# A group norm unit that loads three streams: centred values and a bonus made in the projections

## The chip, the cores and the metric

The kernel runs on one core of a Trainium2 chip. The metric is the device time of one execution in microseconds (us), the median of three runs.

## The reference

One layer of a bidirectional encoder over 1024 tokens of width 1024: a SwiGLU FFN, a mixing layer, and a second FFN, each between RMS norms. The mixing layer projects once and splits into eight attention heads and eight RWKV-7 heads of 64 features. The RWKV part, cut to what matters here:

```python
u = u + mu_prev * (prev - u) + mu_next * (nxt - u)
r, k, v, wd, ad, gd = split(u)
a = sigmoid(a0 + einsum('bsdr,drc->bsdc', ad, a2))          # two directions d
g = sigmoid(gd) @ g2
kk = normalised(k * k_k)                                     # per head
k_dir = k[:, :, None, :] * (1.0 + (a - 1.0) * k_a)
ys = scan(step, state0, (r, decay, k_dir, v, kk, kk * a))    # forward and backward
#   sa = state @ kk;  state = state * w - sa kka^T + v k^T;  y = state @ r
y = ys[:, :, 0] + flip(ys[:, :, 1])
mu = mean(y); var = mean((y - mu) ** 2)                      # per head of 64
y = (y - mu) * rsqrt(var + GN_EPS) * lnx_w + lnx_b
bonus = einsum('bshn,bsdhn,hn->bsh', r, k_dir, r_k) / 2
y = (y + bonus * v) * g
```

The state's rows belong to the value features, and the output of a head is linear in its values. So a value that has its mean over the 64 features taken away ahead of the scan gives an output that has its mean taken away.

## The kernel before

All data is feature-major where a name has `[128, 2, FB]` or `[4, 128, S]`: 128 partitions hold two heads of 64, four such pairs make the eight heads, and tokens run along the row. Instructions are placed on each engine's queue by a scheduler that works from its own cost model and the order of the program as priority; each queue then runs strictly in that order on the chip. SP's queue carries most loads and stores, POOL's (gpsimd) some stores, ACT's a few. A tile of a pool is reused after all its readers are done; `bufs` says how many copies a tag has.

The stages, in the order of the program:

1. First FFN, low-rank projections (decay and in-context rate, stored in `lr_d["w"]` and `lr_d["a"]` per direction, the backward one stored in its own, reversed order of time), values of the attention.
2. Attention, on `ps_a` and `attw`. Behind it in priority stand the projections of `project_rwkv`, column tile by column tile (`ct`): 0 to 3 are receptances r, 4 to 7 keys k, 8 to 11 values v. Each makes 48 products into the PSUM tile `zr`, is shifted (`shift`, tiles `u` and `us`) and goes through `stream`. `ct` 0 is done earlier; then the list is 4, 5, 6, 7, 1, 2, 3. A key's stream squares it, sums per head by small products (`kn`), takes a root and a reciprocal, spreads that by a copy, transposes it back (`kt`) and stores k and the normalised kk. r, k and kk lie together in `rk_d[12]`. A value's stream stores v for the bonus (`v_d`) and, both in order and reversed (`vrev`), transposes it with the identity and stores it token-major in `vt_d` by way of the tile `vts`, which has two buffers.
3. `prep(n)` makes the operands of one block of 128 tokens in both directions: it loads the block's decay and rate (`th_w`, `th_a`) and all twelve rows of `rk_d` in one DMA (`in3`, one buffer), makes `pr`, `bk`, `lm` and `bt`, and stores the direction's key `kd` to `kd_d`. `solve(n)` inverts small triangular matrices on VectorE, step by step in tile `Ti` (lines 866 and 868). prep(0), solve(0), values 8 and 9, prep(1), solve(1), values 10 and 11 follow one another in the program.
4. The scan: `merge` and `chain` for eight blocks of two chunks, with prep and solve of later blocks and the output projection of the attention (`project_attended`) between them. A chunk's output goes to `y_d`.
5. `finish_half` for two halves of two blocks of 256 tokens, each with two units (`finish_unit`, g = 0, 1): a unit covers four heads and 256 tokens. It loads seven tiles (`f_y0`, `f_y1`, `f_k0`, `f_k1`, `f_r`, `f_v`, `f_sg`, shown in views as f_y, f_k, f_r, f_v, f_sg), three buffers each, from a pool that opens when the last prep and solve are done. It adds both directions, centres by a product with `cen` (`yc`), squares, sums (`var`), takes the root, spreads and transposes it (`rstd`), makes the bonus from k, r and v (`bonus`), the gate (`gate`), and writes the unit's result as two parts, high and low (`xh`, `xl`). Its PSUM tiles come from one tag with three buffers.
6. `out_weights` loads eight 256 KB blocks of the output weights through the single buffer `wor` and splits each into `woh` (ACT) and `wol` (VectorE). `out_project` multiplies (`pw`) and `done` normalises each row tile, stores it, and hands it to the second FFN. These steps stand behind stage 5 in priority, but run as their operands come.
7. Second FFN.

Of the kernel before, what the change touches and what calls it, by code (L numbers as in the profile page):

```python
# [10 lines left out]
F32 = mybir.dt.float32  # L11
F32R = mybir.dt.float32r
AF = mybir.ActivationFunctionType
OP = mybir.AluOpType
# [149 lines left out]
class _Kernel:  # L164
# [401 lines left out]
    def stream(self, p, psum, ct, y):  # L566
# [10 lines left out]
        elif ct < 8:  # L577
# [15 lines left out]
            for half in range(2):  # L593
# [5 lines left out]
                V.scalar_tensor_tensor(kr[:, o], y[:, o], g, q, op0=OP.mult, op1=OP.mult)  # L599
            self.nc.gpsimd.dma_start(self.rk_d[8 + i], kr)  # L600
        else:
            i = ct - 8
            self.nc.gpsimd.dma_start(self.v_d[i], y)
            back = p.tile([128, S], F32, name="vrev", tag="us")
            V.tensor_copy(back, y[:, ::-1])
            for src, dst in ((y, self.vt_d[0]), (back, self.vt_d[1])):
                for g in range(2):
                    q = psum.tile([128, 4, 128], F32, name="vt", tag="t")
                    for j in range(4):
                        t = g * 4 + j  # L610
                        T.transpose(q[:, j, :], src[:, t * 128:(t + 1) * 128], self.ident)
                    vt = p.tile([128, 4, 2, 64], F32, name="vts", tag="vts")
                    A.activation(vt.rearrange("p a b c -> p a (b c)"), q, AF.Copy)
# [169 lines left out]
    def prep(self, n, p, psum, big):  # L783
# [8 lines left out]
        for d in range(2):  # L792
# [29 lines left out]
            V.tensor_tensor(bk[:, :, :, C:2 * C], chunks(kd), ei, op=OP.mult)  # L822
            self.nc.sync.dma_start(self.kd_d[d][:, :, ls].rearrange("a p t -> p a t"), kd)
            bt = big.tile([128, BLK, 2, 4, 64], F32, name="bt", tag=f"bt{d}")
# [149 lines left out]

    def finish_unit(self, p, psum, b, g, x, g2w):

        nc, V, A, G, T = self.nc, self.nc.vector, self.nc.scalar, self.nc.gpsimd, self.nc.tensor
        pos = self.blocks.index(b)
        half, cols = pos // 2, slice(pos % 2 * FB, pos % 2 * FB + FB)
        ps2, ts = slice(2 * g, 2 * g + 2), slice(b * FB, (b + 1) * FB)  # L980
        back = slice(S - (b + 1) * FB, S - b * FB)
        z = {}
        for nm, src, sl in (("y0", self.y_d[0], ts), ("y1", self.y_d[1], back), ("k0", self.kd_d[0], ts),
                            ("k1", self.kd_d[1], back), ("r", self.rk_d, ts), ("v", self.v_d, ts)):
            z[nm] = p.tile([128, 2, FB], F32, name="f_" + nm, tag="f_" + nm)
            self.load(z[nm], src[ps2, :, sl].rearrange("a p t -> p a t"))
        sg = p.tile([128, FB], F32, name="f_sg", tag="f_sg")
        self.load(sg, self.sg_d[:, ts])
        y, sq, k, v = z["y0"], z["y1"], z["k0"], z["v"]
        flat = lambda q: q.rearrange("p a t -> p (a t)")  # L990
        bank = lambda nm: psum.tile([128, 2, FB], F32, name=nm, tag="d")

        yc = bank("yc")
        G.tensor_tensor(y, y, z["y1"][:, :, ::-1], op=OP.add)
        T.matmul(yc, self.cen, y, start=True, stop=True)
        A.activation(sq, yc, AF.Square)
        G.tensor_tensor(k, k, z["k1"][:, :, ::-1], op=OP.add)
        for j in range(2):
            V.scalar_tensor_tensor(k[:, j, :], k[:, j, :], self.rkc[:, 2 * g + j:2 * g + j + 1], z["r"][:, j, :],
                                   op0=OP.mult, op1=OP.mult)  # L1000
# [11 lines left out]
        rb = bank("rstd")  # L1012
        for u in range(4):
            T.transpose(flat(rb)[:, u * 128:(u + 1) * 128], flat(sq)[:, u * 128:(u + 1) * 128], self.ident)
        A.activation(y, yc, AF.Copy)
        V.tensor_tensor(y, y, rb, op=OP.mult)
        for j in range(2):
            i = 2 * g + j
            A.activation(y[:, j, :], y[:, j, :], AF.Identity, scale=self.lnw[:, i:i + 1], bias=self.lnb[:, i:i + 1])
        V.scalar_tensor_tensor(v, bs, 0.5, v, op0=OP.mult, op1=OP.mult)  # L1020
        V.tensor_tensor(y, y, v, op=OP.add)
        gt = bank("gate")
        for j in range(2):
            i = 2 * g + j
            T.matmul(gt[:, j, :], g2w[:, i * 128:(i + 1) * 128], sg, start=True, stop=True)
# [9 lines left out]
    def finish_half(self, p, psum, half, x):  # L1035
        g2w = self.load_g2(p)
        for b in self.blocks[2 * half:2 * half + 2]:
            for g in range(2):
                self.finish_unit(p, psum, b, g, x, g2w)

# [58 lines left out]
    def constants(self):  # L1099
# [17 lines left out]
        self.sg_d = self.dram("sg", [128, S])  # L1117
        self.rk_d, self.v_d = self.dram("rk", [12, 128, S]), self.dram("v", [4, 128, S])
        self.q_d, self.kt_d = self.dram("q", [4, 128, S]), self.dram("kt", [4, 128, S])
        self.vt_d = self.dram("vt", [2, S, 2, 4, 64])  # L1120
        self.kd_d = [self.dram(f"kd{d}", [4, 128, S]) for d in range(2)]
        self.y_d = [self.dram(f"y{d}", [4, 128, S]) for d in range(2)]
# [3 lines left out]
    def mix_columns(self):  # L1126
# [36 lines left out]
    def run(self):  # L1163
# [5 lines left out]
        with self.top as top:  # L1169
# [266 lines left out]
```

## Time and profile before

| | |
|---|---|
| Median of three runs | 2369.29 us (2369.18 to 2370.75) |
| Span of the profiled execution, first to last instruction | 2367.7 us, 39507 instructions |
| TensorE busy | 2212.2 us, 93% |
| VectorE busy | 1782.8 us, 75% |
| ScalarE busy | 1034.4 us, 44% |
| GpSimd busy | 608.7 us, 26% |
| DMA | 386.04 MB, mean 163 GB/s |

The profile holds one execution. Its own time is known by its span alone; 1.6 us of the median lie outside that span. A row of the timeline has start, duration, engine, line, operation and tiles (out<-in), and in brackets how long the engine stood idle before it and what released it. PE is TensorE's matmul, PEld its weight load, DVE is VectorE, ACT ScalarE, POOL GpSimd, and SPq or ACTq a DMA issued from that queue. A row of the windows table has the stretch, its length, the busy time of PE, PEld, DVE, ACT and POOL with the number of instructions, the granted TensorE clock, the DMA engines' busy share and GB/s. A row of a group ends with the busy time, the mean ns of one, and the idle time before it with its releasers. A row of the DMA view has the number of issues, KB of each and the median us to landing.

### The profile page before, as it was taken

The page shows a single profiled execution, that of the slowest core. Times are in us where ns is not written, and L with a number is a line of the kernel's source. Part 1 is how long each engine was busy: PE and PEld are TensorE (multiplying, and loading weights), DVE is VectorE, ACT ScalarE, POOL GpSimd, SP SyncE. Part 2 cuts the span into 40 slices and gives each one's busy share as a digit, 9 for nine tenths or more (in the row PEclk, how much of TensorE's full clock was granted, in tenths as well). Part 3 has the DMA queues.
Part 4 walks back from the last instruction along what each step waited for, and adds up shares of the span by engine and source line. Part 5 has one row for each costly group of instructions (what it writes and reads, how often), then busy time and mean ns, then how long its engine had stood idle before and what let it go on. Part 6 is the DMA issues. An engine that isn't in the chain of part 4 may idle for free. (4 is left out here: it accounts for less than half of the span.)

```text
span 2367.7 us, 39507 instructions
## 1 busy us (share of the span) xinstructions
PE 2212.2 (93%) x14532; PEld 1784.9 (75%) x14532; DVE 1782.8 (75%) x2957; ACT 1034.4 (44%) x1958; POOL 608.7 (26%) x732
## 2 busy tenths in 40 slices
PE   6999999999999998999995889988799999999997
PEld 4788888878877676788774767765678888887886
DVE  8899999865676344667568767837889999987565
ACT  4322333354676413666545545445442333235453
POOL 6244443400000010111102242432334344441000
PEclk8999999999999998999996798989989999999999
DMA  5354445486652514322369676577534544447655
GB/s 156 107 174 151 170 146 170 167 266 193 220 185 98 193 42 134 91 81 71 94 161 223 165 183 176 151 208 256 178 95 168 174 167 154 169 153 265 195 188 181
DMA packets 359381, 386.04 MB, mean 163 GB/s; under 512 B 74258, under 2 KB 265618, under 8 KB 359188
## 3 DMA queue, kind: packets, MB, share of 16 engines
q1 hardware_dynamic: 308512, 276.43, 38.8%
q0 software_dynamic: 30320, 94.44, 11.3%
q10 hardware_dynamic: 20356, 12.66, 1.9%
q8 instruction: 114, 1.87, 0.3%
q14 instruction: 79, 0.65, 0.1%
HBM read 257.53 MB, written 125.89 MB: 162 GB/s over the span
## 5 line engine op out<-in xcount | busy, mean ns | idle before, releaser
L186 ACT ACTIVATE wh<-raw 128x512 fp32r<-128x512 f32 (+1 forms) x273 | 167.8, 626 | 264.1 <-DVE raw L62 95.0
L187 DVE TENSOR_TENSOR wl<-raw,wh 128x512 fp32r<-128x512 f32 (+1 forms) x273 | 277.6, 1020 | 3.1 <-ACT wh L186 2.0
L81 PE MATMUL gu<-xh,wh 128*128 128x512 f32 x704 | 277.9, 395 | 0.9 <-ACT xh L186 0.8
L81 PE MATMUL gu<-xl,wh 128*128 128x512 f32 x704 | 276.3, 393 | 0.0
L81 PE MATMUL gu<-xh,wl 128*128 128x512 f32 x704 | 276.2, 392 | 0.0
L415 PE MATMUL pd<-gl,gwh 128*128 128x512 f32 x616 | 240.4, 390 | 3.1 <-DVE gl L187 3.1
L415 PE MATMUL pd<-gh,gwh 128*128 128x512 f32 x616 | 239.6, 390 | 0.5 <-DVE row L86 0.5
L415 PE MATMUL pd<-gh,gwl 128*128 128x512 f32 x616 | 239.7, 389 | 0.0
L86 DVE TENSOR_TENSOR row<-gu,row 128x512 f32<-128x512 f32 x308 | 206.4, 682 | 23.2 <-PE gu L81 22.4
L187 DVE TENSOR_TENSOR gwl<-graw,gwh 128x512 fp32r<-128x512 f32 (+1 forms) x176 | 117.0, 667 | 129.7 <-ACT gwh L186 127.5
L116 POOL DMA_DIRECT2D d_hid<-row x154 | 84.7, 551 | 470.6 <-DVE row L114 444.2
L186 ACT ACTIVATE gwh<-graw 128x512 fp32r<-128x512 f32 (+1 forms) x176 | 101.4, 576 | 190.5 <-PE pd L415 162.2
L81 PEld LDWEIGHTS gu<-xh,wh 128*128 128x128 f32 x704 | 133.9, 190 | 29.5 <-ACT xh L186 2.0
L81 PEld LDWEIGHTS gu<-xl,wh 128*128 128x128 f32 x704 | 133.8, 190 | 27.9
L81 PEld LDWEIGHTS gu<-xh,wl 128*128 128x128 f32 x704 | 133.3, 189 | 27.5
L415 PEld LDWEIGHTS pd<-gl,gwh 128*128 128x128 f32 x616 | 115.6, 188 | 28.5 <-DVE gl L187 4.9
L415 PEld LDWEIGHTS pd<-gh,gwh 128*128 128x128 f32 x616 | 115.5, 188 | 25.6 <-DVE row L86 0.8
L415 PEld LDWEIGHTS pd<-gh,gwl 128*128 128x128 f32 x616 | 115.6, 188 | 23.8
L94 ACT ACTIVATE row<-row 128x512 f32<-128x512 f32 x44 | 27.9, 633 | 223.9 <-DVE row L86 216.4
L187 DVE TENSOR_TENSOR gl<-raw,gh 128x512 fp32r<-128x512 f32 x160 | 112.9, 717 | 15.7 <-ACT gh L186 15.4
L145 POOL TENSOR_TENSOR ws<-ws 128x512 f32<-128x512 f32 x88 | 114.4, 1300 | 1.2
L186 ACT ACTIVATE gh<-raw 128x512 fp32r<-128x512 f32 x160 | 98.0, 621 | 32.2 <-DMA raw<-in_ffn_w_down_dram 21.1
(356 smaller groups left out, 5353.4 us busy)
## 6 DMA issues: line engine op xcount, KB each, us to landing
d_hid<-row POOLq DMA_DIRECT2D x154, 256.0 KB, 2.5
graw<-d_hid SPq DMA_DIRECT2D x132, 256.0 KB, 3.0
raw<-in_ffn_w_gate_dram SPq DMA_DIRECT2D x88, 256.0 KB, 3.1
raw<-in_ffn_w_up_dram SPq DMA_DIRECT2D x88, 256.0 KB, 3.3
ws<-in_ffn_w_down_dram SPq DMA_DIRECT2D x88, 256.0 KB, 4.5
d_ws<-ws POOLq DMA_DIRECT2D x88, 256.0 KB, 2.3
raw<-d_ws SPq DMA_DIRECT2D x88, 256.0 KB, 2.7
raw<-in_ffn_w_down_dram SPq DMA_DIRECT2D x66, 256.0 KB, 3.3
```

Source lines behind the costliest of these rows:

```text
L81: self.K.nc.tensor.matmul(ps, a[:, k, :], b[:, k, :], start=(k == 0 and i == 0), stop=(k == 3 and i == 2))
L86: add = lambda o, x: V.tensor_tensor(o, ps, x, op=OP.add)
L94: A.activation(y[:, 0], y[:, 0], AF.Silu)
L116: put = lambda n, y: G.dma_start(self.hid[n - 1, j // 2], y)
L145: G.tensor_tensor(o, a, b, op=OP.subtract)
L186: self.nc.scalar.activation(h, src, AF.Copy)
L187: (eng or self.nc.vector).tensor_tensor(l, src, h, op=OP.subtract)
L415: T.matmul(ps[x], a[:, ts], b, start=(m == 0 and k == 0), stop=(m == NM - 1 and k == 2))
```

## The change

Values are centred per head on their way to the scan: the transposition with the identity becomes a product with `cen`, which transposes and centres in one step. The bonus is made in the streams of the keys, in two halves of 512 tokens: both directions' rates and the stored r are loaded, r times k times the averaged rate term is summed per head by a product with `ones2` scaled by `r_k`, and the result goes to `bn_d`. For this the receptances now come ahead of the keys. The values' streams load it back, multiply by v and store the product to `bv_d` in place of v. `prep` no longer stores the direction's key. A group norm unit loads y of both directions and `bv`; it neither centres nor makes a bonus, it joins scale, root and shift in two VectorE operations per pair of heads, and the gate's input is loaded once for two units.

```diff
@@ stream, keys
             self.nc.gpsimd.dma_start(self.rk_d[8 + i], kr)
+            for half in range(2):
+                o, ob = slice(half * 512, half * 512 + 512), slice(512 - half * 512, 1024 - half * 512)
+                a0, a1 = (p.tile([128, 512], F32, name="ba", tag="vts") for n in range(2))
+                r = p.tile([128, 512], F32, name="br", tag="br", bufs=1)
+                self.load(a0, self.lr_d["a"][0][i, :, o])
+                self.load(a1, self.lr_d["a"][1][i, :, ob])
+                self.load(r, self.rk_d[i, :, o])
+                V.tensor_tensor(a0, a0, a1[:, ::-1], op=OP.add)
+                A.activation(a0, a0, AF.Identity, scale=self.kaq[:, i:i + 1], bias=self.ka1[:, i:i + 1])
+                V.tensor_tensor(r, r, y[:, o], op=OP.mult)
+                V.tensor_tensor(r, r, a0, op=OP.mult)
+                q = psum.tile([128, 512], F32, name="bn", tag="t")
+                T.matmul(q, self.onesrk[:, i], r, start=True, stop=True)
+                A.copy(a1, q)
+                self.load(self.bn_d[i, :, o], a1)
@@ stream, values
-            self.nc.gpsimd.dma_start(self.v_d[i], y)
+            for half in range(2):
+                o = slice(half * 512, half * 512 + 512)
+                bn = p.tile([128, 512], F32, name="br", tag="br", bufs=1)
+                self.load(bn, self.bn_d[i, :, o])
+                V.tensor_tensor(bn, bn, y[:, o], op=OP.mult)
+                self.nc.gpsimd.dma_start(self.bv_d[i, :, o], bn)
...
-                        T.transpose(q[:, j, :], src[:, t * 128:(t + 1) * 128], self.ident)
+                        T.matmul(q[:, j, :], src[:, t * 128:(t + 1) * 128], self.cen, start=True, stop=True)
@@ prep
-            self.nc.sync.dma_start(self.kd_d[d][:, :, ls].rearrange("a p t -> p a t"), kd)
@@ finish_unit
-        for nm, src, sl in (("y0", self.y_d[0], ts), ("y1", self.y_d[1], back), ("k0", self.kd_d[0], ts),
-                            ("k1", self.kd_d[1], back), ("r", self.rk_d, ts), ("v", self.v_d, ts)):
+        for nm, src, sl in (("y0", self.y_d[0], ts), ("y1", self.y_d[1], back), ("bv", self.bv_d, ts)):
...
-        sg = p.tile([128, FB], F32, name="f_sg", tag="f_sg")
-        self.load(sg, self.sg_d[:, ts])
...
-        yc = bank("yc")
         G.tensor_tensor(y, y, z["y1"][:, :, ::-1], op=OP.add)
-        T.matmul(yc, self.cen, y, start=True, stop=True)
-        A.activation(sq, yc, AF.Square)
-        G.tensor_tensor(k, k, z["k1"][:, :, ::-1], op=OP.add)
-        for j in range(2):
-            V.scalar_tensor_tensor(k[:, j, :], k[:, j, :], self.rkc[:, 2 * g + j:2 * g + j + 1], z["r"][:, j, :],
-                                   op0=OP.mult, op1=OP.mult)
+        A.activation(sq, y, AF.Square)
...
-        bs = bank("bonus")
-        T.matmul(bs, self.ones2, k, start=True, stop=True)
...
-        A.activation(y, yc, AF.Copy)
-        V.tensor_tensor(y, y, rb, op=OP.mult)
-        for j in range(2):
-            i = 2 * g + j
-            A.activation(y[:, j, :], y[:, j, :], AF.Identity, scale=self.lnw[:, i:i + 1], bias=self.lnb[:, i:i + 1])
-        V.scalar_tensor_tensor(v, bs, 0.5, v, op0=OP.mult, op1=OP.mult)
-        V.tensor_tensor(y, y, v, op=OP.add)
         gt = bank("gate")
         for j in range(2):
             i = 2 * g + j
             T.matmul(gt[:, j, :], g2w[:, i * 128:(i + 1) * 128], sg, start=True, stop=True)
+        rb = bank("rstd")
+        for u in range(4):
+            T.transpose(flat(rb)[:, u * 128:(u + 1) * 128], flat(sq)[:, u * 128:(u + 1) * 128], self.ident)
+        for j in range(2):
+            i = 2 * g + j
+            V.scalar_tensor_tensor(y[:, j, :], y[:, j, :], self.lnw[:, i:i + 1], rb[:, j, :], op0=OP.mult, op1=OP.mult)
+            V.scalar_tensor_tensor(y[:, j, :], y[:, j, :], self.lnb[:, i:i + 1], bv[:, j, :], op0=OP.add, op1=OP.add)
@@ finish_half
+            sg = p.tile([128, FB], F32, name="f_sg", tag="f_sg", bufs=2)
+            self.load(sg, self.sg_d[:, b * FB:(b + 1) * FB])
...
@@ mix_columns
+        self.kaq = p.tile([128, 4], F32, name="kaq")
+        G.tensor_scalar(self.kaq, self.kac, 0.25, None, op0=OP.mult)
@@ mix_constants
+        self.onesrk = p.tile([128, 4, 128], F32, name="onesrk")
+        for i in range(4):
+            self.nc.scalar.activation(self.onesrk[:, i], self.ones2, AF.Copy, scale=self.rkc[:, i:i + 1])
@@ run
-            self.project_rwkv(zr, pz, x, [(ct, 1) for ct in (4, 5, 6, 7, 1, 2, 3)])
+            self.project_rwkv(zr, pz, x, [(ct, 1) for ct in (1, 2, 3, 4, 5, 6, 7)])
```

More of the change, by code (lines that the diff above doesn't have):

```diff
@@ L972, in chain, with finish_unit @@
             self.nc.scalar.dma_start(self.y_d[d][:, :, ls].rearrange("a p t -> p a t"), YB[d])
-    def finish_unit(self, p, psum, b, g, x, g2w):
+    def finish_unit(self, p, psum, b, g, x, g2w, sg):
         nc, V, A, G, T = self.nc, self.nc.vector, self.nc.scalar, self.nc.gpsimd, self.nc.tensor
@@ L982, in finish_unit @@
         z = {}
-        for nm, src, sl in (("y0", self.y_d[0], ts), ("y1", self.y_d[1], back), ("k0", self.kd_d[0], ts),
-                            ("k1", self.kd_d[1], back), ("r", self.rk_d, ts), ("v", self.v_d, ts)):
+        for nm, src, sl in (("y0", self.y_d[0], ts), ("y1", self.y_d[1], back), ("bv", self.bv_d, ts)):
             z[nm] = p.tile([128, 2, FB], F32, name="f_" + nm, tag="f_" + nm)
             self.load(z[nm], src[ps2, :, sl].rearrange("a p t -> p a t"))
-        sg = p.tile([128, FB], F32, name="f_sg", tag="f_sg")
-        self.load(sg, self.sg_d[:, ts])
-        y, sq, k, v = z["y0"], z["y1"], z["k0"], z["v"]
+        y, sq, bv = z["y0"], z["y1"], z["bv"]
         flat = lambda q: q.rearrange("p a t -> p (a t)")
         bank = lambda nm: psum.tile([128, 2, FB], F32, name=nm, tag="d")
-        yc = bank("yc")
         G.tensor_tensor(y, y, z["y1"][:, :, ::-1], op=OP.add)
-        T.matmul(yc, self.cen, y, start=True, stop=True)
-        A.activation(sq, yc, AF.Square)
-        G.tensor_tensor(k, k, z["k1"][:, :, ::-1], op=OP.add)
-        for j in range(2):
-            V.scalar_tensor_tensor(k[:, j, :], k[:, j, :], self.rkc[:, 2 * g + j:2 * g + j + 1], z["r"][:, j, :],
-                                   op0=OP.mult, op1=OP.mult)
+        A.activation(sq, y, AF.Square)
         vs = psum.tile([128, 4, 2], F32, name="var", tag="d")
@@ L1009, in finish_unit @@
                      AF.Copy)
-        bs = bank("bonus")
-        T.matmul(bs, self.ones2, k, start=True, stop=True)
-        rb = bank("rstd")
-        for u in range(4):
-            T.transpose(flat(rb)[:, u * 128:(u + 1) * 128], flat(sq)[:, u * 128:(u + 1) * 128], self.ident)
-        A.activation(y, yc, AF.Copy)
-        V.tensor_tensor(y, y, rb, op=OP.mult)
-        for j in range(2):
-            i = 2 * g + j
-            A.activation(y[:, j, :], y[:, j, :], AF.Identity, scale=self.lnw[:, i:i + 1], bias=self.lnb[:, i:i + 1])
-        V.scalar_tensor_tensor(v, bs, 0.5, v, op0=OP.mult, op1=OP.mult)
-        V.tensor_tensor(y, y, v, op=OP.add)
         gt = bank("gate")
@@ L1037, in finish_half @@
         for b in self.blocks[2 * half:2 * half + 2]:
+            sg = p.tile([128, FB], F32, name="f_sg", tag="f_sg", bufs=2)
+            self.load(sg, self.sg_d[:, b * FB:(b + 1) * FB])
             for g in range(2):
-                self.finish_unit(p, psum, b, g, x, g2w)
+                self.finish_unit(p, psum, b, g, x, g2w, sg)
     def out_weights(self, p, k0, gain=None):
@@ L1117, in constants @@
         self.sg_d = self.dram("sg", [128, S])
-        self.rk_d, self.v_d = self.dram("rk", [12, 128, S]), self.dram("v", [4, 128, S])
+        self.rk_d, self.bn_d, self.bv_d = self.dram("rk", [12, 128, S]), self.dram("bn", [4, 128, S]), self.dram("bv", [4, 128, S])
         self.q_d, self.kt_d = self.dram("q", [4, 128, S]), self.dram("kt", [4, 128, S])
         self.vt_d = self.dram("vt", [2, S, 2, 4, 64])
-        self.kd_d = [self.dram(f"kd{d}", [4, 128, S]) for d in range(2)]
         self.y_d = [self.dram(f"y{d}", [4, 128, S]) for d in range(2)]
```

## The prediction

> **What bounds the kernel now.** I read the windows table first, in stretches that follow the stages, to see which engine is full where the change works.
>
> ```profile
> core 0: us, PE busy (x) PEld busy (x) DVE busy (x) ACT busy (x) POOL busy (x), PEclk, DMA share, GB/s
> 1150.00:1190.00 40.00, 38.95 (x270) 31.06 (x270) 23.10 (x64) 19.02 (x52) 6.74 (x12) 1.00 0.32 95
> 1190.00:1240.00 50.00, 44.87 (x295) 36.05 (x294) 30.08 (x60) 25.70 (x55) 1.86 (x3) 0.97 0.65 169
> 1240.00:1290.00 50.00, 30.56 (x189) 24.27 (x187) 43.72 (x130) 23.59 (x44) 14.34 (x23) 0.75 0.90 215
> 1560.00:1594.00 34.00, 25.57 (x482) 20.65 (x478) 5.75 (x13) 13.81 (x25) 11.01 (x11) 0.80 0.92 286
> 1594.00:1650.00 56.00, 45.98 (x191) 28.99 (x190) 38.36 (x65) 30.34 (x61) 13.88 (x11) 0.94 0.79 263
> 1650.00:1700.00 50.00, 46.34 (x219) 37.35 (x217) 43.80 (x61) 26.61 (x55) 8.40 (x6) 1.00 0.51 168
> ```
>
> The end of the attention (1150 to 1190) is full of TensorE work. The start of the scan (1240 to 1290) is full on VectorE. From 1560 to 1650, at the scan's end and in the group norm, no engine is full but the DMA engines are, at 0.92 and 0.79 of their time.
>
> Next the chain of work that ended last, from there to the second FFN:
>
> ```profile
> 1668.36 1.28 DVE row L266
> ...
> 1672.00 2.88 DMA d_h<-row
> 1674.97 1.28 DVE row L266
> ...
> 1752.35 389.02 PE gu L81 x1716
> ```
>
> After the group norm the eight row tiles pass one by one, 1674.97 - 1668.36 = 6.6 us each, because a row is stored (2.88 us) before it is changed in place; then TensorE is the bound to the end. Nothing there is touched. So what counts is when the first row tile can start. Its steps are in the timeline by engine:
>
> ```profile
> 1570.41 0.59 ACT L1083 COPY yao<-po 128x512 f32<-128x512 f32 x1 [10.13 <-DMA d_hp<-yao]
> 1593.73 0.98 ACTq L972 DMA_DIRECT2D d_y<-yb  x2
> 1591.74 0.47 SPq L182 DMA_DIRECT2D wor<-in_w_out_dram  x1
> ...
> 1629.41 0.33 SPq L182 DMA_DIRECT2D wor<-in_w_out_dram  x1
> 1633.86 0.33 SPq L182 DMA_DIRECT2D wor<-in_w_out_dram  x1
> 1638.60 0.33 SPq L182 DMA_DIRECT2D wor<-in_w_out_dram  x1
> 1644.47 0.69 DVE L187 TENSOR_TENSOR wol<-wor,woh 128x512 fp32r<-128x512 f32 x1
> 1649.75 1.04 ACT L244 ACTIVATE junk<-row 128x1024 f32<-128x1024 f32 x1
> ```
>
> The scan's last output leaves at 1593.7. The eight blocks of the output weights go through one buffer, load, ACT half, DVE half, from 1591.74 to 1645.16: 53.4 us, 6.7 each. The quickest turns, with the queues clear, are 1633.86 - 1629.41 = 4.45 and 1638.60 - 1633.86 = 4.74 us. The first row tile starts (L244) 4.6 us after the last weight. So the weights' ring ends last here, and it is slow because its loads and its two conversions stand in SP's, ACT's and DVE's queues among the norm units.
>
> **The group norm, the gain.** The DMA view of 1558 to 1650 and a group of 1594 to 1650:
>
> ```profile
> f_y<-d_y SPq DMA_DIRECT2D x16, 256.0 KB, 4.4
> f_k<-d_kd SPq DMA_DIRECT2D x16, 256.0 KB, 4.9
> f_r<-d_rk SPq DMA_DIRECT2D x8, 256.0 KB, 5.7
> f_v<-d_v SPq DMA_DIRECT2D x8, 256.0 KB, 3.8
> wor<-in_w_out_dram SPq DMA_DIRECT2D x8, 256.0 KB, 3.9
> L999 DVE SCALAR_TENSOR_TENSOR f_k<-f_k,rkc,f_r 128x256 f32<-128x256 f32 x8 | 3.7, 480 | 5.0 <-POOL f_k L997 5.0
> ```
>
> The f_k, f_r and f_v loads go, 32 of 256 KB, and f_bv brings 8: 24 fewer, 6.3 MB, at the 263 GB/s of the windows row 24 us of DMA time. Four f_sg loads go too. Per unit POOL loses one of its two adds, DVE loses L999 (2 x 0.48) and three 512-wide operations and gains four 256-wide ones of 0.48, ACT loses a copy and two affine steps. TensorE loses the centring and the bonus product, which I price from the gate:
>
> ```profile
> 1593.22 0.66 PE L1014 MATMUL rstd<-ident,f_y 128*128 128x128 f32 x4
> 1593.71 1.03 PE L1025 MATMUL gate<-f_sg,g2w 128*128 128x256 f32 x4
> 1594.58 1.02 PE L995 MATMUL yc<-f_y,k_cen 128*128 128x512 f32 x2
> ```
>
> Four transposes occupy 1593.71 - 1593.22 = 0.49 us, a 512-column fp32 product 1594.58 - 1593.71 = 0.87. With less in all four queues I let the ring turn in 4.6 us (the mean of the quick turns): 8 x 4.6 = 37 instead of 53.4, so 16.6 us earlier. A few more come from its start: the 1591.74 load stood on SP behind f_k and f_r loads for later units, which no longer exist. I add 3.4 for that: **-20 us**. Bounds: 14 (all turns at 4.74 with one lost, no earlier start) to 28. The norm units don't end last after that: three tiles of PSUM per unit replace five, in a pool of three, so one unit needs about the gate, rstd and four DVE steps, some 4 to 5 us, against 7.
>
> The 10.13 us that ACT stood behind a store at 1570.41 I leave as it is: the loads issued ahead of that store are about as many after the change.
>
> **The projections, the cost.** The order becomes 1 to 7, so the last stream ahead of prep(0) is a key instead of a receptance.
>
> ```profile
> 1125.52 1.15 ACT L583 ACTIVATE ksq<-us,c_rwkv_k_k 128x1024 f32<-128x1024 f32 x1 [0.88 <-DVE us L525]
> 1129.21 1.28 ACT L589 ACT_TABLE_LOAD   x1
> 1140.21 0.53 POOL L600 DMA_DIRECT2D d_rk<-kr  x1 [13.67 <-DVE kr L599]
> 1190.62 0.53 POOL L576 DMA_DIRECT2D d_rk<-us  x1 [9.35 <-DVE us L525]
> 1194.09 0.38 SPq L182 DMA_DIRECT2D in<-d_rk  x1
> 1200.63 0.69 DVE L810 TENSOR_TENSOR pr<-in,e 128x512 f32<-128x512 f32 x1 [3.36 <-DMA in<-d_rk]
> 1269.21 0.17 DVE L868 TENSOR_TENSOR Ti<-Ti,ttmp 128x16 f32<-128x16 f32 x1
> 1277.23 0.53 POOL L860 MEMSET Ti<- 128x512 f32 x1 [3.60 <-DMA d_t<-Ti]
> ```
>
> Now the last receptance is stored at 1190.62, the joint load of r, k and kk goes at 1194.09, and prep(0) begins at 1200.63. A key's norm takes 1140.21 - 1125.52 = 14.7 us inside the attention. Outside it two table loads of 1.28 and the exponentials between its steps fall away; I take 9. On SP that load holds back the zraw loads queued after it and prep(0)'s DMAs.
>
> Eight bonus products of 0.87 are 7 us on a full TensorE; six come ahead of the last key, while that key's own norm products (about 2 us) now come after it: +3. So prep(0) starts 12 us later. It doesn't all reach the scan: DVE idles 20 of the 50 us from 1190 to 1240, and the value streams, which need no prep, fill the wait; I let 4 come back. The scan's gate is POOL at 1277.23, which waited for the solve that ended at 1269.4, so what is left passes on: **+8 us**, bounds 0 and 14.7.
>
> The other edits there: the bonus needs 24 loads and 8 stores of 256 KB on SP and 24 DVE steps of 0.69 (16.6 us), beside the attention where DVE has 17 of 40 us and DMA two thirds free; if that cover were gone it is the slower rival below. In the value streams eight products of 0.69 (5.5 us) and bn loads, with the v store split in two on POOL, fall partly where DVE is full; I count them in the +8. The centring turns 64 transposes into products: 0.12 to 0.22 by the rows above, 6 us on TensorE between 1206 and 1277, which idles 19 of 50 us in 1240 to 1290: nothing. The Trainium skill, in "TensorE: Matmul & The Clock Gate", Terms, says fp32 is four times faster in the transpose mode. By that rule the 64 would cost about 23 us, a rival below; the rows show a factor of two.
>
> **The scan.** The sixteen kd stores go.
>
> ```profile
> th_a<-d_a SPq DMA_DIRECT2D x16, 256.0 KB, 5.5
> d_kd<-th_a SPq DMA_DIRECT2D x16, 256.0 KB, 2.7
> ```
>
> They stood on SP behind DVE steps and ahead of the loads of the next prep, and held th_a for 2.7 us: **-2 us**, between 0 and -5. Constants (four ACT copies, one POOL scale) cost nothing: they lie ahead of the attention, where ACT is far from full.
>
> **Sum.** The span is 2367.7 us and the median of the runs 2369.3, 1.6 above it, which I keep. +8 - 2 - 20 = -14: **2355 us**; with the bounds of all three, 2336 to 2370.
>
> **The rivals.** *The weights start early (2339).* If SP gets to the first wor load when the attention's weights are done, near 1575, ring and first units end just behind the scan and the gain is 36: 2369.3 + 8 - 2 - 36. For it: the first four units need no output of the last chunk. Against it: the queues' order is fixed beforehand, and ACT and DVE are in the chain then. By the Trainium skill, "DMA: Bandwidth & Descriptors", Anatomy of one DMA, a transfer takes 2 us plus its bytes over 436 GB/s, an estimate of 2.6 us for 256 KB alone, where wor took 3.9; by that rule eight quicker loads would give some 10 us more.
>
> *The ring stays slow (2370).* If the weights still stand behind the units' conversions and a turn takes 6.0, the gain is 5. For it: the slow turns of the ring waited on ACT and DVE as well as on SP.
>
> *The bonus ring starts late (2379).* Its a tiles share two buffers with the value streams' vts tiles.
>
> ```profile
> L613 ACT ACTIVATE vts<-vt x16: 578/598/604, 1206.5 to 1277.6; 128x512 f32<-128x512 f32 x16
> ```
>
> One half costs a load 5.5 + add 0.69 + ACT 0.59 + product 0.69 + TensorE 0.87 + copy 0.59 + store 2.7 = 11.6 us, a key 23, four keys 93. The store waits on SP for the copy, and the next columns' zraw loads stand behind it. If these chains begin only as the attention ends near 1164, they end at 1257 and the sixteen vts follow: 40 us at 10 a stream ends 20 after 1277.6, the old pace of 71 us ends 50 after. At +32: 2369.3 + 32 - 2 - 20. It decides from a scan start 27 us late. Against it: the fourth projection was done at 1125, so at least one bonus lies in the attention, and loads can run ahead.
>
> *The dearer transposes (2360).* 23 us go into 1206 to 1277, where by the windows rows TensorE idles some 18 (5.1 x 34/50 and 19.4 x 37/50): +5 on the scan start.
>
> **How the numbers follow.** My forecast 0.50 (of it 0.45 faster, 0.05 same), early weights 0.15 (all faster), slow ring 0.13 (0.03, 0.06, 0.04 slower), late bonus 0.17 (0.03 same, 0.14 slower), dearer transposes 0.05 (0.04, 0.01). 0.2% is 4.7 us, about what a measurement of this kernel can tell from no change. Faster 0.67, same 0.15, slower 0.18. The range 2336 to 2380 leaves out the outer parts of the first and third rivals. The forecast's own range is 2343 to 2368.
>
> **What would show it.** Right: the first wor load to the last wol in under 42 us, the first L244 of that stage some 12 us earlier (20 less the 8), DMA share from 1600 on below 0.6, prep(0)'s first L810 near 1212 and the first chunk of the scan near 8 us late. Wrong: a scan start more than 25 us late with ACT's vts waiting on bonus tiles; a ring still at 6 us a turn; or L995's replacement, the vt products, at 0.4 us each.

## The result, and the profile after

The changed kernel is slower: 2450.38 us (median of 4 runs, 2449.22 to 2462.07) against 2370.02 us on the same chip, a ratio of 1.0355 with a 95% interval of 1.0331 to 1.0380. The prediction was 2355 us with 2336 to 2380 as its range: wrong in sign, and 70 us beyond the range. The profiled execution has a span of 2447.4 us, 79.7 more than the 2367.7 of before.

The extra time lies in three places. The first is one where nothing was changed. These are windows rows (PE busy and instructions first, granted clock and DMA share at the end) of the two FFNs, before and then after:

```profile
120.00:440.00 320.00, 320.00 (x1413) 265.08 (x1412) 312.73 (x339) 96.74 (x169) 141.88 (x165) 1.00 0.48 164
1880.00:2120.00 240.00, 240.00 (x1061) 198.79 (x1060) 233.04 (x255) 73.06 (x126) 103.77 (x121) 1.00 0.47 161
```

```profile
120.00:440.00 320.00, 320.00 (x1373) 257.04 (x1372) 303.71 (x327) 94.18 (x161) 139.41 (x162) 1.00 0.45 156
1880.00:2120.00 240.00, 240.00 (x1030) 192.79 (x1029) 226.28 (x252) 71.87 (x123) 98.21 (x115) 1.00 0.46 155
```

TensorE is busy all the time at a granted clock of 1.00 in all four rows, yet it starts 1373 products instead of 1413 in 320 us: 3% fewer, in code that the diff does not touch. The chain of waits shows the same in the second FFN, 1814.59 to 2215.70 here against the 389.02 us for practically as many products that the prediction shows:

```profile
1814.59 401.11 PE gu L81 x1719
```

The second place is the start of the scan. The timeline of ScalarE has the end of the fourth projection and the first half of the fifth (L523), the first and the last copy of a bonus (L614), the first value tile (L633) and, at the end, the scan's last output and the first row tile:

```profile
1141.49 0.68 ACT L523 ACTIVATE us<-zr,mu 128x512 f32<-128x512 f32 x1
1179.19 0.69 ACT L523 ACTIVATE us<-zr,mu 128x512 f32<-128x512 f32 x1
1181.63 0.59 ACT L614 COPY ba<-bn 128x512 f32<-128x512 f32 x1 [0.55 <-PE bn L613]
...
1268.60 0.59 ACT L614 COPY ba<-bn 128x512 f32<-128x512 f32 x1 [0.17 <-PE bn L613]
1276.85 0.60 ACT L633 ACTIVATE vts<-vt 128x512 f32<-128x512 f32 x1
...
1658.34 0.65 ACT L989 COPY yb<-y 128x256 f32<-128x256 f32 x2 [2.17 <-PE y L956]
1716.19 1.04 ACT L244 ACTIVATE junk<-row 128x1024 f32<-128x1024 f32 x1
```

All eight halves of the bonus come after the attention (it ends at 1180.1), one every (1268.60 - 1181.63) / 7 = 12.4 us, and the first value tile (`vts`) follows the last of them. That is 70.3 us later than the 1206.5 of before; the attention itself ended only 16 us later.

The third place is where the gain was to come from. From the scan's last output to the first row tile it takes 57.9 us here (1716.19 - 1658.34) and took 56.4 before (1593.33 to 1649.75). The loads did go, f_bv in place of f_k, f_r and f_v, but a wor load still goes only once in 7.5 us ((1706.85 - 1662.09) / 6) and the DMA share of this stage is 0.78 (0.79 before). The windows row, two lines of the DMA view and the wor loads in SP's timeline:

```profile
1659.00:1715.00 56.00, 40.37 (x149) 29.74 (x149) 33.73 (x67) 19.58 (x37) 9.93 (x9) 0.70 0.78 260
```

```profile
f_bv<-d_bv SPq DMA_DIRECT2D x8, 256.0 KB, 6.2
wor<-in_w_out_dram SPq DMA_DIRECT2D x8, 256.0 KB, 4.3
```

```profile
1662.09 0.35 SPq L182 DMA_DIRECT2D wor<-in_w_out_dram  x1
...
1702.82 0.33 SPq L182 DMA_DIRECT2D wor<-in_w_out_dram  x1
1706.85 0.33 SPq L182 DMA_DIRECT2D wor<-in_w_out_dram  x1
```

### The profile page after: what moved, and what is told of

It is laid out like the page before. It is cut to its first block, busy times and chain, and to the rows that moved or that the text cites. A ratio compares the mean times of both kernels' runs of the same rounds, so it can differ in the third digit from the quotient of the medians.

```text
span 2447.4 us, 39645 instructions
## 1 busy us (share of the span) xinstructions
PE 2288.7 (94%) x14580; PEld 1815.7 (74%) x14580; DVE 1790.9 (73%) x2981; ACT 1037.7 (42%) x1950; POOL 600.5 (25%) x729
```

## The experiments

Each ratio is against the kernel before on the same chip; 0.001 is 2.4 us. By the intervals a difference of two ratios is known to about 8 us. Medians of different chips are not compared. The edits are shortened.

**Where the tiles lie.** Of all that the change does, one thing reaches the first FFN: kaq, 16 bytes a partition, lies in the pool of constants at the bottom of the left stack (the program lays its pools out in two stacks, left and right) and moves every tile above it up, by 32 bytes (e11 below, which moves the other stack by 32, bears that number out). Among them is xh, the operand of the first FFN's products; its weights wh and wl lie on the right stack and stay. Four kernels test it:

```
e1:  + p.tile([128, 4], F32, name="pad")       (unused, where kaq stands)
e2:  + p.tile([128, 128], F32, name="pad")
e11: e1, and tile([128, 120], name="edge") -> tile([128, 112], name="edge")
e12: + p.tile([128, 16], F32, name="pad")
```

> The kernel before with one unused tile of 16 bytes a partition in the pool of constants, at the place where the change puts kaq; no instruction differs. Every tile of the left stack then lies 32 bytes higher, as in the changed kernel. Theory A (the place of the tiles in SBUF slows TensorE's products): the pace of the products from 120 to 440 us falls from 178 to 173 in 40 us, the second FFN's long run of products from 389 to about 401 us, and the time rises by 35 to 50 us (12 in each FFN, 10 to 20 in the stages between). Theory B (the slower pace comes from another part of the change or from the state of the chip): the pace stays at 178 and the time within 5 us of 2369.

> The same unused tile, but of 512 bytes a partition, so that every tile of the left stack lies 512 bytes higher and starts at a multiple of 512 again. Theory A: the pace stays at 178 products in 40 us and the time within 5 us of 2369: what counts is the address within 512 bytes, not that something is moved. If any move slows it, or the schedule that the build makes: +35 to +50 us as with the small tile. Theory B: within 5 us of 2369.

Measured: e1 1.0193 (1.0165 to 1.0221), 46 us slower with no instruction changed; e2 1.0003 (0.9980 to 1.0027). Theory A. Which relation of addresses counts was asked of e11 and e12:

> The kernel before with the unused tile of 16 bytes on the left stack and 32 bytes less in the unused tile at the right edge, so that the tiles of both stacks lie 32 bytes higher. No instruction differs. Theory A1 (what slows a product is that its stationary and its moving operand lie differently within 512 bytes; in the changed kernel gu, zv and pw, with one operand on each stack, take 396 or 397 ns, while zq, with both on the left, still takes 389): the pace is 178 products in 40 us and the time within 8 us of the kernel before. Theory A2 (each operand has to start at a multiple of 512, or of 64, bytes by itself): pace 173 or worse, +43 us or more.

> The kernel before with an unused tile of 64 bytes: the left stack 64 bytes higher, the right one in place. Read by its pace from 120 to 440 us alone: 178 in 40 us (1413 in 320) if 64 bytes is the grain of what counts, 173 (1384) if the grain is coarser.

e11 1.0030 (1.0011 to 1.0050): with both stacks 32 bytes higher, nearly all the loss is gone, and the small rest is not explained here. e12, one execution, 2393.66 us. The products by tile (min/median/max ns): first two rows of before, then gu and zq of e1, gu of e11, gu of e12, and last the windows row of e12:

```profile
L81 PE MATMUL gu<-xh,wh x704: 387/389/796, 22.1 to 2137.8; 128*128 128x512 f32 x176
L440 PE MATMUL zq<-z1h,xh x64: 388/389/505, 801.5 to 852.6; 128*128 128x512 f32 x64
```

```profile
L81 PE MATMUL gu<-xh,wh x704: 388/396/796, 22.4 to 2169.3; 128*128 128x512 f32 x176
L440 PE MATMUL zq<-z1h,xh x64: 387/389/793, 830.2 to 883.0; 128*128 128x512 f32 x64
```

```profile
L81 PE MATMUL gu<-xh,wh x704: 387/389/795, 23.4 to 2151.0; 128*128 128x512 f32 x176
```

```profile
L81 PE MATMUL gu<-xh,wh x704: 387/392/795, 24.7 to 2157.7; 128*128 128x512 f32 x176
```

```profile
120.00:440.00 320.00, 320.00 (x1399) 262.57 (x1398) 309.94 (x335) 96.84 (x169) 140.97 (x163) 1.00 0.46 159
```

In e1, gu has one operand on each stack and takes 396 ns; zq has both on the left, shifted alike, and keeps its 389. In e11 gu has both shifted alike and is back at 389. So what costs is that one operand of a product is shifted against the other, and not the place of either alone. 32 bytes cost 40 of 1413 products, 64 bytes 14, 512 none: neither outcome expected of e12, but one between. At 64 bytes it also depends on the pair: the medians of gu are 392 ns (xh, wh), 394 (xl, wh) and 388 (xh, wl). Why the engine does this no run shows, nor whether 128 or 256 bytes would do as well as 512.

The repair, kaq in the 16 bytes that lie spare behind kah:

```
- kah = tile([128, 4]); kaq = tile([128, 4])
+ kah8 = tile([128, 8]); kah, kaq = kah8[:, :4], kah8[:, 4:]
```

> The changed kernel with kaq in the spare bytes behind kah, so that the left stack lies where it lay before; all else of the change is kept. Theory A: pace back to 178 in 40 us, both FFNs at their old length, 2450 - 35 to 50 = 2400 to 2415 us. What is then left above 2369, 30 to 45 us, belongs to the change itself. Theory B: 2450 within 5 us.

Measured: 1.0133 (1.0111 to 1.0155), 2401.23 us; the changed kernel's ratio was 0.0222 higher, 53 us. The pace is 1413 products again. What follows is built on this version or on the kernel before, as each text says.

**The start of the scan.** The order of the projections alone, the bonus alone taken out, and the bonus with the receptances and keys interleaved:

> The kernel before with the projections in the order 1 to 7 and nothing else, so a key is the last stream ahead of the first preparation. Theory C (the bonus chains hold the start of the scan back, 87 us of them between 1181 and 1268, and the order by itself costs what the prediction says, at most 9 us of a key's norm): 2369 to 2380 us, the first solve step less than 12 us later than 1237.8. Theory D (the order itself costs most of the 51 us between the attention's end and the first solve step): 2400 us or more.

> The changed kernel with the left stack in its old place, and the bonus left out: no ba, br and bn work in the key streams; the value streams load a key stream's stored tile in place of the bonus, so that their own loads, products and stores stay. Theory C (the bonus chains stand between the attention and the first value stream): first vts about 35 us earlier than with them (1247.7 before that, so 1208 to 1216), time 2401 - 35 = 2366 us, bounds 2358 to 2374. Rival E (the value streams' loads and products, or the centring products, hold the start of the scan back as well): the first solve step stays 15 us or more behind that of the kernel before (1238.1), time 2380 us or more.

> The changed kernel with the left stack in its old place and the projections in the order 4, 1, 5, 2, 6, 3, 7, in which each key still comes after the receptance that its bonus reads. Theory C: the bonus of two keys lies inside the attention, which ends some 12 us later for it, and two keys' chains of 22 us stay behind: the first vts 20 to 30 us earlier than 1247.7, time 2372 to 2385 us. Rival H (TensorE is full in the attention, so what goes in there comes back as its length): within 6 us of 2401.

Measured: e4 1.0013 (0.9992 to 1.0035), no difference that shows; its first solve step came at 1250.3, where e2, with the old order, has 1247.7. e5 0.9968 (0.9944 to 0.9992): the bonus costs 0.0165 of 2370, 39 us, where it stands, and the rest of the change together is worth -7.5 us. Its first value tile comes at 1204.5, that of e3 at 1247.7. e8 1.0090 (1.0060 to 1.0120), 10 us better than e3 and not the 16 to 29 expected: its first value tile comes at 1230.8, 17 us earlier, and two keys' bonus lies in the attention, but that ends at 1165.0 instead of 1150.2. Theory C and rival H each have a share.

What makes a chain slow was asked by loosening it:

```
- br bufs=1;  V.tensor_tensor(r, r, y[:, o]);  T.matmul(q, onesrk[:, i], r);  A.copy(a1, q);  self.load(bn_d, a1)
+ br bufs=2;  V.scalar_tensor_tensor(r, r, rkc[:, i], y[:, o]);  T.matmul(q, ones2, r);  A.copy(r, q);  nc.scalar.dma_start(bn_d, r)
```

> The changed kernel with the left stack in its old place and the bonus chain loosened: two br tiles instead of one (in the room of onesrk, whose factor goes into the product of receptance and key), the copy of the bonus goes into br instead of ba, so both ba tiles come free after the second product, and ScalarE issues the store instead of SP. The work is the same but for four small copies. Theory C1 (the chains are slow because of their single buffers and the store that SP waits for): a half takes about 7 us instead of 12.4, the last bn product comes some 20 us earlier than 1238.9, time 2378 to 2386 us by the scale on which the kernel before is 2369 (ratio 1.004 to 1.007 against 1.0133). Rival C2 (the chain's own steps, one after the other, or TensorE in this stretch, set the pace): ratio 1.011 or more.

Measured: 1.0023 (1.0005 to 1.0042), 26 us better than e3 and better than expected. One turn from the changed kernel's timeline, then one of e9:

```profile
1217.48 0.33 SPq L182 DMA_DIRECT2D d_bn<-ba  x1
1220.73 0.33 SPq L182 DMA_DIRECT2D ba<-d_a  x1
1224.24 0.68 DVE L608 TENSOR_TENSOR ba<-ba 128x512 f32<-128x512 f32 x1
1225.74 0.83 ACT L609 ACTIVATE ba<-ba,ka,kaq 128x512 f32<-128x512 f32 x1
1227.11 0.68 DVE L611 TENSOR_TENSOR br<-br,ba 128x512 f32<-128x512 f32 x1
1229.63 1.02 PE L613 MATMUL bn<-br,onesrk 128*128 128x512 f32 x2
1230.69 0.59 ACT L614 COPY ba<-bn 128x512 f32<-128x512 f32 x1 [4.12 <-PE bn L613]
1231.31 0.32 SPq L182 DMA_DIRECT2D d_bn<-ba  x1
1234.43 0.32 SPq L182 DMA_DIRECT2D ba<-d_a  x1
```

```profile
1194.92 0.58 ACT L614 COPY br<-bn 128x512 f32<-128x512 f32 x1
1195.53 0.35 ACTq L615 DMA_DIRECT2D d_bn<-br  x1
1195.55 1.13 PE L613 MATMUL bn<-br,k_ones 128*128 128x512 f32 x2
1196.71 0.59 ACT L614 COPY br<-bn 128x512 f32<-128x512 f32 x1 [0.72 <-PE bn L613]
```

Above, the load of the next ba goes 3.2 us after the store of this one, since the store still reads the buffer: from 1180 to 1270 SP waited six times for such a store, 12.0 us in all. The steps up to the next copy come behind that load, and each of them stands in its engine's queue among other work. Below, the second half's product starts as soon as the first half's copy is under way: two copies 1.8 us apart, and TensorE is busy 59.5 of the 62 us from 1160 to 1222, where in the changed kernel it was busy 72.9 of the 88 from 1181 to 1269. Which of the three edits (second buffer, copy into br, store from ScalarE's queue) brings how much was not separated.

Where the bonus stands was asked by putting it behind the value streams, made from stored streams, in the old order of projections:

> The changed kernel with the left stack in its old place and the old order of the projections; the bonus is made after the last value stream, from stored streams (loads of both a, r, k and v, eight halves), and only the group norm and the pools that follow on its place wait for it. Theory C (the bonus costs by standing ahead of the value streams): the first solve step within 8 us of 1238.1, time no more than that without any bonus and 10 us: ratio 0.995 to 1.003. Rival I (the work costs its time wherever it stands, or the attended projections, whose tiles come free later, push the scan's end): ratio 1.008 or more.

> The kernel of the run before with four buffers for the raw output weights: 0.3 to 0.6% below it if the ring sets the first row there too, so a ratio of 0.990 to 0.998; the same ratio if the norm units or the scan's last loads set it.

Measured: e14 1.0406 (1.0378 to 1.0433), e15 1.0344 (1.0320 to 1.0369). Theory C missed, rival I held, though by another way than its attended projections. e15 is 0.6% below e14, as expected if the weights' ring sets the first row there too. The waits from 1300 to 1420 and the windows row of e14:

```profile
PEld bn L637 <- DVE br L635: 86.5, 8, 14.0
ACT ba L633 <- DVE ba L631: 79.1, 7, 13.5
```

```profile
1300.00:1395.00 95.00, 17.41 (x26) 4.58 (x24) 48.25 (x134) 12.09 (x18) 12.76 (x23) 0.51 0.50 147
```

TensorE works 17 of 95 us. It and ScalarE stand in front of the eight halves' steps, about 12 us a half, and the scan's first work is queued behind them: the first of its uv products comes at 1419.6 instead of 1312.4. Neither of the two places that were tried for the slow chain was harmless, since the queues run in order.

**The group norm.** Four buffers instead of one for the raw output weights (`bufs=1` to `bufs=4` in the second out_weights), in the aligned kernel, in the kernel before, and with the looser chains without and with the mixed order:

> The changed kernel with the left stack in its old place, and four buffers instead of one for the raw output weights. Theory F (the ring of one buffer is what keeps the group norm's gain from showing: its eight turns of 6.9 us end at 1679.4, 6.7 us after the last norm unit): first row 10 to 16 us earlier, 2385 to 2391 us. Rival G (the norm units themselves, 5.6 us each, set the end): the ring's last turn comes earlier but the first row at most 3 us, 2398 to 2401 us.

> The kernel before with four buffers instead of one for the raw output weights and nothing else. If the ring set the start of the row tiles there, as the prediction read it (first load 1591.7, last conversion 1644.5, first row 1649.8): 10 to 18 us faster, 2352 to 2360 us. If the norm units set it: within 4 us of 2369.

> The looser bonus chains (ratio 1.0023), left stack in its old place, order 1 to 7, and four buffers for the raw output weights. If the ring still sets the first row: from the scan's end to the first row 43 to 46 us instead of 55, ratio 0.995 to 0.998. If the four buffers were what slowed the joint run: 1.004 or more.

> The kernel of the run before, with the projections in the order 4, 1, 5, 2, 6, 3, 7 and four buffers for the raw output weights. If the three gains add up (chains -0.7%, order -0.4%, ring -0.5% on a ratio of 1.0133): ratio 0.994 to 1.000. If order and chains gain the same time twice: 1.000 to 1.005.

Measured: e6 1.0081 (1.0055 to 1.0107), about 12 us better than e3; e7 1.0012 (0.9991 to 1.0032), nothing; e13 1.0004 (0.9984 to 1.0023), not told apart from e9's 1.0023, though its first row tile comes 39.4 us after the scan's last output, earlier than the 43 to 46 expected; e10 1.0052 (1.0026 to 1.0079). The gains do not add up, and e13 puts e10's loss on the mixed order: with chains that keep pace, an order that lengthens the attention (to 1174.5, against 1161.4 in e13) only costs. ScalarE's last weight and first row tile, in e7 and then in e6:

```profile
1609.96 1.65 ACT L186 ACTIVATE woh<-wor 128x512 fp32r<-128x512 f32 x3
1653.62 1.06 ACT L244 ACTIVATE junk<-row 128x1024 f32<-128x1024 f32 x1 [0.76 <-DVE xl L187]
```

```profile
1644.47 0.61 ACT L186 ACTIVATE woh<-wor 128x512 fp32r<-128x512 f32 x1
1670.87 1.05 ACT L244 ACTIVATE junk<-row 128x1024 f32<-128x1024 f32 x1
```

In e7 the last weight is converted at 1611, 33 us earlier than before (1643.8), and yet the first row tile comes 58.9 us after the scan's last output instead of 56.4. That row tile waits for xl, a norm unit's result (in brackets). So in the kernel before the norm units ended as late as the ring did, and the ring alone was not the bound. In the changed kernel it is: e6 needs 43.0 us from the scan's last output (1627.88) to the first row tile, e3 55.3.

**The centring alone.** The value tiles centred and the norm units without their centring, in the kernel before; with four buffers; and the other way round, e13 with the centring undone:

> The kernel before with the centring part of the change alone: the value products take the centring matrix, the norm units lose the centring product, one copy and the two affine steps on ScalarE, and two of their DVE steps become four of half the width; bonus, kd stores, order and loads as before. Theory: the units end last in the kernel before (four buffers gained nothing there), each gets about 1 us shorter (0.87 product, 0.6 copy and 1.2 affine steps, against nothing added), but the ring of one buffer at 6.6 to 6.9 us a turn stands right behind them: -2 to -6 us, ratio 0.9975 to 0.999. Rival: the 64 value products, 0.33 instead of 0.22 us, stand in the start of the scan: +2 to +7 us.

> The same with four buffers for the raw output weights, so that neither the units' old length nor the ring holds the first row: scan's end to first row 47 to 52 us instead of 56.6, -5 to -10 us, ratio 0.996 to 0.998. Rival: as long as the units load eight tiles the DMA engines hold them, and nothing more comes: the ratio of the run before.

> The kernel with looser bonus chains and four buffers (ratio 1.0004), but with the centring part undone: value tiles are transposed with the identity, and a norm unit has its centring product and one copy again. If the centring's cost at the start of the scan (0.3% alone) is what counts: ratio 0.996 to 0.999, a version faster than both kernels. If what it saves in the norm units is worth as much once the bonus no longer loads there: 1.000 to 1.003.

Measured: e16 1.0031 (1.0012 to 1.0049), the rival; e17 1.0013 (0.9992 to 1.0033), not the -5 to -10 us expected, though its first row tile did come 51.2 us after the scan's end, inside the 47 to 52; e18 1.0000 (0.9977 to 1.0023), not told apart from e13. The value products by tile and the first row of them in TensorE's timeline, before and in e16 (the half from us; that from vrev is alike):

```profile
L611 PE MATMUL vt<-ident,us x32: 270/273/476, 1205.6 to 1267.9; 128*128 128x128 f32 x32
1205.64 0.66 PE L611 MATMUL vt<-ident,us 128*128 128x128 f32 x4 [2.67 <-DVE us L525]
```

```profile
L611 PE MATMUL vt<-k_cen,us x64: 274/276/580, 1208.7 to 1277.5; 128*128 128x128 f32 x64
1208.67 1.16 PE L611 MATMUL vt<-k_cen,us 128*128 128x128 f32 x8 [1.69 <-DVE us L525]
```

A product leaves two records of 0.276 us where a transpose leaves one of 0.273. Records overlap, so what counts is the row: four products take 1.16 us and four transposes 0.66, half a microsecond more for each of the sixteen value tiles, some 8 us. From the first value tile to the scan's first uv product it takes 112.6 us in e16 and 112.4 in e17, and 104.1 to 106.3 in six kernels with transposes and the same program up to there (before, e1, e2, e7, e11, e12): 6 to 8.5 us later, about the 7 us of the ratio. At the end the centring does gain: the last row tile comes 111.8 us after the scan's last uv product in e16 and 107.6 in e17, against 114.3 to 118.4 in those six. The start of the scan takes that back. None of the versions is faster than the kernel before by more than its interval, but for e5, which leaves the bonus out.

## Why the prediction was wrong, point by point

The ratio of 1.0355 splits as 0.0222 for the place of the tiles (1.0355 - 1.0133), 0.0165 for the bonus (1.0133 - 0.9968) and -0.0032 for all the rest: of 2370 us that is 53, 39 and -7.6, together 84, where the medians lie 80 apart. Of the signs that the prediction named for being wrong two came, a scan start more than 25 us late and a ring above 6 us a turn.

**Constants cost nothing** is the step that failed first and cost most. It counted the instructions of the new constants and not their room: 16 bytes at the bottom of the left stack cost 53 us (46 in e1, by itself) in stages that the prediction left out of its sum. No rival named it either. The unused tiles called edge, of 480 and 448 bytes, were in view in the code, as a sign that the place of the tiles had been set on purpose.

**The bonus beside the attention.** The rival of the late ring named the mechanism, and gave it 0.17: chains on shared buffers that begin only as the attention ends, 11.6 us a half (measured 12.4), 93 us in all (87 from first to last copy), deciding from a scan start 27 us late. In the aligned kernel (e3) the first uv product is 41 us late, 1353.5 against 1312.4; before, then e3:

```profile
L937 PE MATMUL st<-uv,bt x512: 217/222/369, 1312.4 to 1592.1; 128*64 128x64 f32 x171
L956 PE MATMUL st<-uv,bt x512: 222/222/370, 1353.5 to 1628.4; 128*64 128x64 f32 x171
```

What was held against it, that the fourth projection was done at 1125 so at least one bonus lies in the attention, is the failed argument. In the new order the fourth projection is the first key, and it ended at 1141. These are the last step ahead of its first bonus product, the last step of its norm, and that product:

```profile
1148.83 0.68 DVE L611 TENSOR_TENSOR br<-br,ba 128x512 f32<-128x512 f32 x1
1179.21 0.74 DVE L599 SCALAR_TENSOR_TENSOR kr<-us,c_rwkv_k_k,kt 128x512 f32<-128x512 f32 x1
1180.57 1.02 PE L613 MATMUL bn<-br,onesrk 128*128 128x512 f32 x2
```

The operand was ready at 1149.5, and the product came 31 us later, with the attention over. It stands behind the key's norm in TensorE's queue and shares the norm's only PSUM buffer (`bn` and `kt` both have the tag t); the norm's steps in turn stood among the attention's, with TensorE busy 38.0 of the 39 us from 1141 to 1180. Whether the queue or the buffer held the product longer was not tried. The cover was counted on VectorE and the DMA engines, which had room, and not by the places in the queues and buffers; a chain on single buffers needs start and end times.

**The start of the scan, +8.** Without the bonus it was +5 (1317.4 in e5), and the order alone costs at most 8 us by its interval. Counted from the first product of the projections, e5 takes 393.5 us to there and six kernels with the old program up to there 386.8 to 392.3, so without the chains this term was not far off, but hardly told from nothing.

**The scan, -2.** From the first to the last uv product 280.7 us before, 275.8 in e3. Nine kernels that keep the kd stores take 268.0 to 287.3 us for it, so these traces neither bear this term out nor refute it.

**The group norm, -20.** The units did get shorter; a ring at 4.6 us a turn did not come. ScalarE's halves of it in e3:

```profile
L186 ACT ACTIVATE woh<-wor x8: 612/617/630, 1631.1 to 1679.4; 128x512 fp32r<-128x512 f32 x8
```

Its turns are (1679.4 - 1631.1) / 7 = 6.9 us, since the load, ScalarE's half and VectorE's half still stand between the steps of the units in three queues. The last row tile, counted from the scan's last uv product, comes 107.7 us later in e3 and 116.0 before (114.3 to 118.4 in six kernels with the old units): the gain is 8 us, and four buffers make it 11.7 (1731.9 - 1627.6 = 104.3 in e6). The first row tile gained 1 us and then 13. That it is what counts, with the row tiles following at a fixed pace, is a second step that failed: from the first to the last row tile it takes 59.4 us before, 52.1 in e3 and 61.0 in e6. In e18 the first row comes 8 us earlier than in e13, and the last no earlier (102.7 us after the last uv product against 101.4). What holds the later rows then was not isolated; in e6 TensorE is busy 41.6 of the 45 us from 1680, about when the last norm unit ends, to 1725. The prediction's 2.6 us for a load, by the Trainium skill, "DMA: Bandwidth & Descriptors", Anatomy of one DMA, rests on a fit that this section gives for transfers issued from GpSimd; wor goes by SP's queue and took 4.3 us after the change.

**The dearer transposes** cost the forecast nothing, and as a rival +5 for the scan's start, with a chance of 0.05. The forecast's 6 us on TensorE were about right (some 8 by the rows of e16); that they would vanish in TensorE's idle time was wrong, since the scan's start came 6 to 8.5 us later. The rival's +5 came near that by luck: it was what 23 us leave beyond the idle time, and nothing like 23 us was added. The Trainium skill, in "TensorE: Matmul & The Clock Gate", Terms, has the transpose mode four times faster in fp32; these rows show two records against one, and 1.16 us against 0.66 for a value tile, a factor of 1.8 to 2, as the prediction's own rows had it.

## What to carry to other kernels

Before an edit is priced by its instructions, list which tiles it moves: a few bytes in a pool that lives to the end shift everything above, and a stage that no line of the diff touches can pay for it; in spare bytes of an existing tile the same constant cost nothing here. Work that is to be hidden needs its chain laid out by buffers (when does the buffer come free, who issues the next load) and by its place in each in-order queue, since an engine that is free on average still waits in front of the chain's next step. When two things end at the same time, as the weights' ring and the norm units did here, test each with the other made free before a gain is put on either.

## What was not expected of the hardware

A TensorE product of 512 columns took 396 instead of 389 ns when one of its operands was shifted by 32 bytes against the other, 388 to 394 at 64 bytes, 389 when both were shifted alike. In 119 runs of the kernel before, on four chips, the span went from 2353.8 us at a mean granted clock of 0.967 to 2380.4 at 0.953, with a correlation of -0.85, about 15 us for 0.01 of clock; which of the two follows the other is not shown, but a difference of a few us between two single profiles is not read as an effect here.
